# Two kernels in one program: where the load of the expert biases and the branch for crowded experts stand

## The chip, the cores and the metric

The kernel runs on one core of one Trainium2 chip. A core has a matrix engine (TensorE, PE in the profile), three elementwise engines (VectorE or DVE, ScalarE or ACT, GpSimd or POOL), a queue processor that here issues every DMA (SyncE, SP), an on-chip memory (SBUF) and accumulators (PSUM). Inputs and weights lie in HBM. The metric is the device time of one execution in microseconds (us); lower is better.

## The reference

256 tokens of width 1024 pass through two blocks in float32. The first block (four attention and convolution branches, then a gated feed-forward network) and the front of the second (pooling, differential attention, cross attention) are not touched by the change. The second block ends in a mixture of experts, and that is where the change lies:

```
logits = xt @ w_router + b_router                     # 256 tokens, 32 experts
top_val, top_idx = top_k(logits, 4); gates = softmax(top_val)
for each expert e, for the tokens xb that chose it:
    hb = clamped_swiglu(xb @ w_gu[e] + b_gu[e])       # w_gu[e]: 1024 x 2048
    yb = hb @ w_down[e] + b_down[e]                   # w_down[e]: 1024 x 1024
    y[token] += yb * gate
return rms_norm(x + y)
```

Each expert has 12 MB of weights, all 32 have 384 MB, and every one of them is read once.

## The kernel before

The work before the experts ends with the cross attention: its output product against `w_co` is added into `x_t` (the residual stream, 128 x 2 x 1024, kept on chip), the router's logits are taken, and `x_t` is added into the four PSUM accumulators `acc` (`seed`, L1337). `x_t` has no other use after that, and its space serves the experts: columns 0 to 1023 of the flat view `xa` hold an expert's gate and up values (`gs`), 1024 to 1535 its product `u_`, and the last 256 columns, `bd4`, take the down biases of all experts, which `load_b_down` brings by four small DMAs (L1422). So that load has to wait until `seed` and the scaling on POOL (L1346) have read `x_t`.

Weights come in pieces of 1 MB. A piece lies in a slot of 8 KB per partition; there are 23 slots, and the string `SLOTS` gives the order in which `slot_tile` (L1481) hands them out, round and round. An expert takes 8 pieces for gate and up (`load_gu`) and 4 for down (`load_dn`). The first two pieces of expert 0 are loaded much earlier, and 382 are left. Most slots lie on memory that the cross attention used, so the first round through the string waits for its last readers: slot h for the scores (L1225), the slots p for the splits of `w_co` (L185), d, e, i and j for the values (L1251), c for the output product (L201), b and a for the router (L1307, L1301). From the second round on a slot waits for the product that read it. The first 34 pieces are chained, each issued behind the one before (`in_turn`, L1489); the bias load is outside that chain. SP issues in order: while its first instruction waits, nothing behind it starts. Each DMA also waits until the one eight places earlier has landed.

A planner sets the order on each engine: of the instructions that it thinks ready, the one that comes first in the program goes first.

A loop runs over the experts. In the turn of expert e the gate and up product of expert e+1 is made (`front`, L1529), with the other half of the swiglu of e and the scatter of e-1 between its eight steps, and then the down product of e (L1571), which for an even e is interleaved with the gather of tokens for the next two experts. Each expert has room for 64 tokens. For experts with more there is `overflow`: a loop over all experts inside a branch, `tc.If(most > CAP)`, L1615. With these inputs no expert has more, so the loop is skipped; still each engine loads the count, branches, and on the skip path waits until its own earlier work is complete and raises its semaphores to what the other path would leave. On SP this means that all DMAs issued before have landed (eight queue semaphores). Nothing that stands behind the branch in the program is moved ahead of it, and the other way round. In the kernel before the branch stands behind all weight loads, behind the scatter of expert 29 and ahead of the swiglu of expert 30.

Of the kernel before, what the change touches and what calls it, by code (L numbers as in the profile page):

```python
# [11 lines left out]
F32 = mybir.dt.float32  # L12
# [10 lines left out]
P = 128  # L23
T = 256
D = 1024
DFF = 2816
NFC = DFF // P
NE = 32
# [15 lines left out]
def kernel(ctx: ExitStack, tc: tile.TileContext, A, out, probe=None, stop=None):  # L44
# [45 lines left out]
    def ps(name, tag="mm"):  # L90
        return pst["pool"].tile([P, 512], F32, tag=tag, name=name, bufs=pst["tags"][tag])
# [174 lines left out]
    def half(h):  # L266
        return slice(h * 512, (h + 1) * 512)
# [1047 lines left out]
    if stopped("cross"):  # L1315
# [9 lines left out]
    slots = {c: ctx.enter_context(tc.tile_pool(name=f"raw_{c}", reuse_waits="tile", bufs=1))  # L1325
             for c in sorted(set(SLOTS) - set("px"))}
# [93 lines left out]
    def load_b_down():  # L1420
        for q in range(4):
            ld(bd4[q * NE:(q + 1) * NE, :], A["b_down_2"][0, :, q * 256:(q + 1) * 256])  # L1422

    def add_b_down(odd):

        g4 = small.tile([P, 2, 4, NE], F32, tag="SG", name="g4", bufs=1)
        V.tensor_copy(g4, gate.unsqueeze(2).to_broadcast([P, 2, 4, NE]))
        gT = xa[:, 1024:1280]
        pt = ps("gT_ps", "tr")
        for b in range(2):  # L1430
            PE.transpose(pt[:, b * P:(b + 1) * P], g4[:, b].rearrange("p q e -> p (q e)"), ident)
        V.tensor_copy(gT, pt[:, :T])
        for b in range(2):
            for h in range(2):
                q = 2 * h + odd
                rows_ = slice(q * NE, (q + 1) * NE)
                PE.matmul(acc[b][h][:, odd * 256:(odd + 1) * 256], gT[rows_, b * P:(b + 1) * P], bd4[rows_, :],
                          start=False, stop=False, tile_position=(q * NE, 0))

    def one_hot(pos_cols, n, name, s_=None):  # L1440

        if s_ is None:
            s_ = small.tile([P, 2, n, 2, CAP], BF16, tag="S_", name=f"S{name}")
        io = iota_s.unsqueeze(1).unsqueeze(1).to_broadcast([P, n, 2, CAP])
        for b in range(2):
            pos = pos_cols[:, b, :].unsqueeze(2).unsqueeze(3).to_broadcast([P, n, 2, CAP])
            last["V"] = V.tensor_tensor(s_[:, b], io, pos, op=ALU.is_equal)
        return s_
# [34 lines left out]
    def slot_tile():  # L1483

        rawc[0] += 1
        pool = slots[SLOTS[slot[0] % len(SLOTS)]]
        slot[0] += 1
        return pool.tile([P, 2 * D], F32, tag="raw", name=f"raw{rawc[0]}")
# [13 lines left out]
    def dn_piece(src, k, t):  # L1502

        t = t.rearrange("p (k c) -> p k c", k=2)
        in_turn(t, src[2 * k * P:(2 * k + 2) * P, :].rearrange("(k p) c -> p k c", p=P))
        return t

    def load_gu(src, ahead=()):
        return [*ahead, *(gu_piece(src, k, slot_tile()) for k in range(len(ahead), 8))].__getitem__

    def load_dn(src, halves=False):
        w = [dn_piece(src, k, slot_tile()) for k in range(4 - halves)]
        if halves:
            t = slot_tile().rearrange("p (k c) -> p k c", k=2)
            for i in range(2):
                ld(t[:, i, :], src[(6 + i) * P:(7 + i) * P, :])
            w.append(t)
        return w.__getitem__
# [14 lines left out]
    def gu_out(pgu, name, gs=None):  # L1533
        if gs is None:
            gs = xa[:, :D]
        for n in range(2):
            S.copy(gs[:, n * 512:(n + 1) * 512], pgu[n])  # L1537
        return gs
# [36 lines left out]
    def scatter(stop=False, after=None):  # L1575

        for b in range(2):
            for y in (yh, yl):
                for h in range(2):
                    rows_ = slice(h * CAP, (h + 1) * CAP)  # L1580
                    PE.matmul(acc[b][h], sT[rows_, b * P:(b + 1) * P], y[rows_, :], start=False,  # L1581
                              stop=stop and y is yl)
            if after:
                after(b)


    GR = 2
    st = {}

    def group(g):  # L1590
        st["S", g] = one_hot(pos1[:, :, g * GR:(g + 1) * GR], GR, f"g{g}")
        st["xg"], chunk = gather(st["S", g], GR, f"g{g}")
        return chunk

    def front(e, between):
        w = load_gu(w_gu[e], () if e else gu0)
        pgu = gu_product(w, st["xg"], (e % GR) * CAP, f"e{e}", between)

        gs = slots["i"].tile([P, 2 * D], F32, tag="raw", name="gs_i")[:, :D] if e == NE - 2 else None
        return gu_out(pgu, f"e{e}", gs)  # L1600

    def slots_of(e):
        g, o = divmod(e, GR)
        st["gslot", e] = turn_slots(st["S", g][:, :, o], gate3[:, :, e, :], f"e{e}")

    chunk = group(0)
    gs = front(0, {k: [lambda k=k: chunk(k + 1)] if k else [lambda: chunk(0), lambda: chunk(1)] for k in range(7)})
    with behind({"V": last["V"]}):
        gates()
    load_b_down()  # L1610


    def overflow():
        most = nc.values_load(cnt_i[0:1, NE:NE + 1], min_val=0, max_val=T)
        with tc.If(most > CAP):  # L1615
            with tc.For_i(0, NE, 1) as e:
                ne = nc.values_load(cnt_i[0:1, bass.ds(e, 1)], min_val=0, max_val=T)
                with tc.If(ne > CAP):
                    pc = small.tile([P, 2, 1], F32, tag="pc", name="pc", bufs=1)
                    gc = small.tile([P, 2, 3], BF16, tag="gc", name="gc", bufs=1)  # L1620
                    bc = small.tile([P, 16], F32, tag="bc", name="bc", bufs=1)
                    V.tensor_copy(pc, pos1[:, :, bass.ds(e, 1)])
                    V.tensor_copy(gc, gate3[:, :, bass.ds(e, 1), :].rearrange("p b o q -> p b (o q)"))
                    V.tensor_copy(bc, bgu[:, :, bass.ds(e, 1)].rearrange("p c o -> p (c o)"))
                    wsl = [slots[c].tile([P, 2 * D], F32, tag="raw", name=f"wsl{c}") for c in "jc"]
                    oxg = work[:, :D // 2].rearrange("p (c s) -> p c s", c=8)

                    os_ = small.tile([P, 2, 1, 2, CAP], BF16, tag="S_", name="os_")

                    def piece(f, src):  # L1630
                        return lambda k: f(src, k, wsl[k % 2])

                    for blk in range(1, T // CAP):
                        V.tensor_scalar(pc, pc, float(CAP), None, op0=ALU.subtract)
                        s_ = one_hot(pc, 1, f"o{blk}", os_)
                        _, chunk = gather(s_, 1, f"o{blk}", oxg)
                        gslot = turn_slots(s_[:, :, 0], gc, f"o{blk}")
                        wg = w_gu[bass.ds(e, 1)].rearrange("o k c -> (o k) c")
                        wd = w_dn2[bass.ds(e, 1)].rearrange("o k c -> (o k) c")
                        g0 = gu_out(gu_product(piece(gu_piece, wg), oxg, 0, f"o{blk}",  # L1640
                                               {k: [lambda k=k: chunk(k)] for k in range(8)}), f"o{blk}")
                        make = swiglu(g0, bc, f"o{blk}")
                        make(0)
                        make(1)
                        dn_product(piece(dn_piece, wd), gslot, f"o{blk}")
                        scatter()

    for e in range(NE - 2):
        make = swiglu(gs, bgu[:, :, e], f"e{e}")
        make(0)  # L1650
        between = {1: [lambda: make(1)], 4: [lambda: slots_of(e)]}
        if e:
            between[3] = [lambda: scatter()]
        gs = front(e + 1, between)
        wd = load_dn(w_dn2[e])
        if e == 2:
            counts()
        chunk = group(e // GR + 1) if e % GR == 0 else None
        dn_product(wd, st["gslot", e], f"e{e}", chunk)
        if e in (2, 4):  # L1660
            add_b_down(e // 2 - 1)


    e0, e1 = NE - 2, NE - 1
    wd0, wg1, wd1 = load_dn(w_dn2[e0]), load_gu(w_gu[e1]), load_dn(w_dn2[e1], halves=True)
    scatter()
    work = slots["e"].tile([P, 2 * D], F32, tag="raw", name="work")
    gb2 = work[:, D:]
    for h in range(2):
        pt = ps(f"gb2_{h}")  # L1670
        for c in range(4):
            PE.matmul(pt[:, c * P:(c + 1) * P], vec["last"][:, 4 * h + c:4 * h + c + 1].to_broadcast([P, P]), ident,
                      start=True, stop=True)
        S.copy(gb2[:, half(h)], pt)
    overflow()
    make = swiglu(gs, bgu[:, :, e0], f"e{e0}")
    make(0)
    make(1)
    slots_of(e0)
    dn_product(wd0, st["gslot", e0], f"e{e0}")  # L1680
    pgu = gu_product(wg1, st["xg"], (e1 % GR) * CAP, f"e{e1}", {1: [scatter]})
    gs = gu_out(pgu, f"e{e1}")
# [50 lines left out]
```

## Time and profile before

| | |
|---|---|
| median of 3 runs | 1735.26 us (1732.9 to 1735.35) |
| the profiled execution | 1734.44 us |
| its span, first to last instruction | 1732.7 us |
| PE busy | 1616.9 us (93%) |
| DVE, ACT, POOL busy | 733.9, 516.5, 232.6 us |
| DMA queue of SP | 526.06 MB |
| mean granted TensorE clock | 0.990 |

A busy PE is not a PE at its peak. The chain of waits follows back from the last instruction and names at each step what released it. SPq, PEq and so on are an engine's instruction queue: semaphore, branch and DMA-issuing instructions. [...]

### The profile page before, as it was taken

Reading aid. Unit: us, or ns where it says so; the run is one execution under the profiler, and the core shown is the slowest. Engines: PE = TensorE matmul, PEld = TensorE weight load, DVE = VectorE, ACT = ScalarE, POOL = GpSimd, SP = SyncE. Lnnn points to the kernel's source line nnn. Section 1 sums busy time; section 2 is a strip of 40 time slices with the busy share of each in tenths; the row PEclk is TensorE's granted clock in tenths of the full one; section 3 lists DMA queues with packets and bytes.
Section 4 is the critical chain, followed back from the end, with each engine's and each line's share of the span. In section 5 each row is a group of like instructions: output and inputs, shape, how many; then the busy total and the mean of one; then the engine's idle time right before and its main releaser. Section 6 shows DMA issues by size and latency. Waiting matters only on the chain.

```text
span 1732.7 us, 24096 instructions
## 1 busy us (share of the span) xinstructions
PE 1616.9 (93%) x9539; PEld 974.3 (56%) x9540; DVE 733.9 (42%) x1606; ACT 516.5 (30%) x973; POOL 232.6 (13%) x332
## 2 busy tenths in 40 slices
PE   8899999999999999989999999998998988899877
PEld 8887799989999788853333333332332233233222
DVE  5867754667777775552122212221222222122122
ACT  4454554555555565531111011100100010011011
POOL 6988312200010000030000000000000000000000
PEclk9999999999999999989999999999999999999989
DMA  9851355664646545529999999999999999999994
GB/s 290 253 170 56 102 183 182 233 199 157 227 147 213 158 130 196 234 108 417 418 414 418 416 418 417 416 418 416 418 415 418 417 417 417 416 418 415 418 414 190
DMA packets 182675, 527.64 MB, mean 305 GB/s; under 512 B 13649, under 2 KB 101758, under 8 KB 149758
## 3 DMA queue, kind: packets, MB, share of 16 engines
q1 hardware_dynamic: 182558, 526.06, 79.2%
q8 instruction: 76, 1.25, 0.3%
q14 instruction: 41, 0.34, 0.1%
HBM read 524.95 MB, written 4.22 MB: 305 GB/s over the span
## 4 chain that ended last, share of the span: by engine, by line
PE 63%; DMA 26%; DVE 6%; ACT 2%; issue 2%; POOL 1%; SPq 0%; DVEq 0%; POOLq 0%; ACTq 0%
DMA raw<-in_w_gu_dram 18%; PE gue L1529 15%; DMA raw<-in_w_down_dram 8%; PE dne L1571 7%; PE dt L201 2%; PE dt L200 2%; PE dt L199 2%; PE xgg L1472 2%; PE g L193 2%; PE g L194 2%; PE g L192 2%; DVE wl L185 2%; PE acc L1581 1%; PE ffv L194 1%; PE ffv L193 1%
## 5 line engine op out<-in xcount | busy, mean ns | idle before, releaser
L1529 PE MATMUL gue<-raw,xgg 128*64 128x512 f32 x2032 | 468.9, 599 | 19.6 <-DMA raw<-in_w_gu_dram 19.6
L185 DVE TENSOR_TENSOR wl<-raw,wh 128x1024 fp32r<-128x1024 f32 (+3 forms) x218 | 273.3, 1255 | 177.5 <-ACT wh L184 177.0
L184 ACT CAST wh<-raw 128x1024 fp32r<-128x1024 f32 (+2 forms) x220 | 227.8, 1035 | 258.1 <-PE g L193 64.3
L1529 PEld LDWEIGHTS gue<-raw,xgg 128*64 128x64 f32 x2032 | 134.0, 136 | 289.4 <-issue 223.1
L1571 PE MATMUL dne<-raw,x_t 128*64 128x512 f32 x1024 | 247.3, 605 | 8.2 <-DMA raw<-in_w_down_dram 6.9
L1476 DVE TENSOR_SCALAR xgg<-xgg,v_c 128x128 f32<-128x128 f32 x120 | 42.1, 351 | 324.0 <-PE gue L1529 194.3
L1537 ACT COPY x_t<-gue 128x512 f32<-128x512 f32 x62 | 36.3, 585 | 341.4 <-PE gue L1529 341.4
L1571 PEld LDWEIGHTS dne<-raw,x_t 128*64 128x64 f32 x1024 | 64.1, 136 | 118.4 <-issue 85.7
L1697 POOL TENSOR_TENSOR ssl<-ssl,nhalf 128x1 f32<-128x1 f32 x2 | 1.1, 563 | 956.9 <-DVE ssl L1696 956.9
L1551 DVE TENSOR_TENSOR x_t<-gte,bgu 128x256 f32<-128x256 f32 x62 | 26.3, 425 | 214.6 <-ACT x_t L1537 165.0
L1472 PEld LDWEIGHTS <-xs 128*128 128x128 bf16 x768 | 46.6, 98 | 103.7 <-issue 101.6
L1472 PE MATMUL xgg<-Sg,xs 128*128 128x128 bf16 x768 | 65.3, 221 | 30.4 <-DVE xgg L1476 25.0
L209 ACT ACTIVATE yh<-dne,gslote 128x512 fp32r<-128x512 f32 x32 | 22.0, 687 | 224.7 <-PE dne L1571 224.7
L379 POOL TENSOR_TENSOR convo<-convo,prod 128x256 f32<-128x256 f32 x90 | 76.9, 854 | 7.4
L192 PE MATMUL g<-h_h,wh 128*128 128x256 f32 x256 | 73.1, 286 | 0.0
L193 PE MATMUL g<-h_l,wh 128*128 128x256 f32 x256 | 73.1, 285 | 0.0
L194 PE MATMUL g<-h_h,wl 128*128 128x256 f32 x256 | 72.9, 285 | 0.0
L1557 ACT ACTIVATE x_t<-x_t 128x256 f32<-128x256 f32 x62 | 25.8, 417 | 155.3 <-DVE x_t L1555 153.0
L378 POOL TENSOR_SCALAR prod<-hconv,v_c 128x256 f32<-128x256 f32 x90 | 66.9, 744 | 8.6
L1553 DVE TENSOR_TENSOR x_t<-gte,bgu 128x256 f32<-128x256 f32 x64 | 26.8, 419 | 79.7 <-PE dne L1571 79.7
L1545 PEld LDWEIGHTS gte<-ident,x_t 128*128 128x128 f32 x248 | 26.0, 140 | 58.3 <-issue 44.1
L194 PE MATMUL ffv<-h_h,wl 128*128 128x256 f32 x176 | 49.9, 284 | 0.2 <-DVE wl L185 0.2
(808 smaller groups left out, 3054.7 us busy)
## 6 DMA issues: line engine op xcount, KB each, us to landing
raw<-in_w_gu_dram SPq DMA_DIRECT2D x254, 1024.0 KB
raw<-in_w_down_dram SPq DMA_DIRECT2D x138, 1024.0 KB
raw<-in_w_in_dram SPq DMA_DIRECT2D x32, 1024.0 KB
raw<-in_w_up_dram SPq DMA_DIRECT2D x22, 1024.0 KB
raw<-in_w_out_dram SPq DMA_DIRECT2D x8, 1024.0 KB
raw<-in_w_ckv_dram SPq DMA_DIRECT2D x8, 1024.0 KB
raw<-in_w_in_dram SPq DMA_DIRECT2D x13, 512.0 KB
raw<-in_w_br_dram SPq DMA_DIRECT2D x12, 512.0 KB
```

The source lines that it names most:

```text
L184: S.copy(hi, src)
L185: last["lo"] = (eng or V).tensor_sub(lo, src, hi.bitcast(F32))
L192: PE.matmul(o, wh[:, k, :], ah[:, k, :], start=first and k == 0, stop=False)
L193: PE.matmul(o, wh[:, k, :], al[:, k, :], start=False, stop=False)
L194: PE.matmul(o, wl[:, k, :], ah[:, k, :], start=False, stop=last and k == nk - 1)
L378: G.tensor_scalar(prod[0][:, :T], hconv[:, c, k:k + T], w, 0.0, op0=ALU.mult, op1=ALU.add)
L379: G.tensor_add(convo[:, c, :], convo[:, c, :], prod[0][:, :T])
L1472: PE.matmul(po[:, :n * CAP], part[:, b, c * P:(c + 1) * P], s_[:, b, :, 0, :], start=i == 0, stop=i == 5)
L1476: V.tensor_scalar(xg[:, c, :], po[:, :n * CAP], vec["ffn"][:, c:c + 1], None, op0=ALU.mult)
L1529: PE.matmul(pgu[n][cg * CAP:(cg + 1) * CAP, :], xg[:, k, col:col + CAP], w[:, cg * D + n * 512:cg * D + (n + 1) * 512], start=k == 0, stop ...
L1537: S.copy(gs[:, n * 512:(n + 1) * 512], pgu[n])
L1571: PE.matmul(po[cg * CAP:(cg + 1) * CAP, :], u_[:, k // 4, k % 4, :], w[:, k % 2, cg * 512:(cg + 1) * 512], start=k == 0, stop=k == 7)
```

## The change

The down biases: `load_b_down()` stands no longer behind the first expert's gate and up product but in the turn of expert 1, behind the loads of its down weights, which is behind 32 pieces.

The branch: `overflow()` stands in the turn of expert 25 (`EOVER`), behind its down product and a scatter of its own, which is left out of the next turn. Pieces of experts 0 to 26 (gate and up) and 0 to 25 (down) are loaded ahead of the branch, the 64 others behind it. Its three tiles and the copy that keeps the gate and up values of the next expert out of its way are taken from the slots in turn instead of by name, and so is the tile for the end of the kernel.

```diff
     GR = 2
+    EOVER = NE - 7
...
-        gs = slots["i"].tile([P, 2 * D], F32, tag="raw", name="gs_i")[:, :D] if e == NE - 2 else None
-        return gu_out(pgu, f"e{e}", gs)
+        return gu_out(pgu, f"e{e}", slot_tile()[:, :D] if e == EOVER + 1 else None)
...
     with behind({"V": last["V"]}):
         gates()
-    load_b_down()
-
     def overflow():
+        wsl = [slot_tile() for _ in range(2)]
+        oxg = slot_tile()[:, :D // 2].rearrange("p (c s) -> p c s", c=8)
         most = nc.values_load(cnt_i[0:1, NE:NE + 1], min_val=0, max_val=T)
...
-                    wsl = [slots[c].tile([P, 2 * D], F32, tag="raw", name=f"wsl{c}") for c in "jc"]
-                    oxg = work[:, :D // 2].rearrange("p (c s) -> p c s", c=8)
...
-        if e:
-            between[3] = [lambda: scatter()]
+        if e and e - 1 != EOVER:
+            between[3] = [scatter]
         gs = front(e + 1, between)
         wd = load_dn(w_dn2[e])
+        if e == 1:
+            load_b_down()
...
         if e in (2, 4):
             add_b_down(e // 2 - 1)
+        if e == EOVER:
+            scatter()
+            overflow()
...
-    work = slots["e"].tile([P, 2 * D], F32, tag="raw", name="work")
+    work = slot_tile()
...
-    overflow()
     make = swiglu(gs, bgu[:, :, e0], f"e{e0}")
```

## Rows read from the trace of the kernel before

**Rows 1.** The page's 40 slices of the span: DMA busy in tenths, and GB/s.

```profile
DMA  9851355664646545529999999999999999999994
GB/s 290 253 170 56 102 183 182 233 199 157 227 147 213 158 130 196 234 108 417 418 414 418 416 418 417 416 418 416 418 415 418 417 417 417 416 418 415 418 414 190
```

**Rows 2.** Waits of SP's queue: us in total, times, longest.

```profile
SPq L1422 <- PE acc L1337: 38.9, 1, 38.9
```

**Rows 3.** Windows (us, engines, PEclk, DMA share, GB/s), 730 to 768 us.

```profile
730.00:732.00 2.00, 2.00 (x12) 1.68 (x11) 1.34 (x2) 1.41 (x3) 0.00 (x0) 1.00 0.42 176
...
734.00:764.00 30.00, 29.48 (x143) 21.08 (x142) 14.87 (x28) 12.39 (x27) 6.96 (x9) 1.00 0.00 1
764.00:768.00 4.00, 1.13 (x9) 0.77 (x9) 3.62 (x7) 1.95 (x4) 3.93 (x5) 0.75 0.09 29
```

**Rows 4.** Timeline of SP, 700 to 812 us: start us, us, what was issued.

```profile
700.11 24.85 SPq L1493 DMA_DIRECT2D raw<-in_w_gu_dram  x6
765.32 1.72 SPq L1422 DMA_DIRECT2D x_t<-in_b_down_dram  x4
767.08 2.07 SPq L1493 DMA_DIRECT2D raw<-in_w_gu_dram  x4
...
772.15 19.41 SPq L1493 DMA_DIRECT2D raw<-in_w_gu_dram  x8
```

**Rows 5.** Lines L1225, L1251, L1307: ns (min/median/max), first and last start.

```profile
L1225 PE MATMUL cs<-mk,cq__7799 x32: 378/379/483, 699.1 to 726.3; 128*128 128x256 f32 x32
...
L1251 PE MATMUL cy<-cpts,mv__3684 x32: 377/379/483, 709.0 to 740.9; 128*128 128x256 f32 x32
...
L1307 PE MATMUL lp<-ident,lsb x4: 193/276/276, 759.1 to 759.3; 128*128 128x32 f32 x4
```

**Rows 6.** Timeline of DVE and of PE, 738 to 754 us.

```profile
746.33 1.22 DVE L185 TENSOR_TENSOR wl<-raw,wh 128x1024 fp32r<-128x1024 f32 x1 [0.58 <-ACT wh L184]
...
753.60 0.39 PE L201 MATMUL dt<-wh,co_l 128*128 128x512 f32 x1
```

**Rows 7.** Chain of waits, first experts: start us, us, what.

```profile
771.52 3.61 PE gue L1529 x8
...
835.30 5.15 PE dne L1571 x24
```

**Rows 8.** Windows, the expert stage as one stretch.

```profile
767.00:1700.00 933.00, 851.91 (x4419) 301.04 (x4420) 213.38 (x601) 99.91 (x198) 3.27 (x3) 0.99 1.02 416
```

**Rows 9.** Chain of waits: down products of experts 8, 10, 24 and 28.

```profile
1033.80 1.87 PE dne L1571 x8
...
1090.03 1.87 PE dne L1571 x8
...
1511.29 1.87 PE dne L1571 x8
...
1633.07 1.87 PE dne L1571 x8
```

**Rows 10.** Line L1615, the branch: ns (min/median/max), first and last start.

```profile
L1615 SPq EVENT_SEMAPHORE  x9: 17/17/17, 1701.9 to 1711.3; - x9
...
L1615 PEldq COMPARE_BRANCH  x1: 6026/6026/6026, 1674.6 to 1674.6; - x1
...
L1615 SPq COMPARE_BRANCH  x1: 45/45/45, 1696.8 to 1696.8; - x1
```

**Rows 11.** Timeline, end of the kernel, PE.

```profile
1681.12 1.09 PE L1545 MATMUL gte<-ident,gs_i 128*128 128x128 f32 x4 [6.36 <-PEq L1615]
...
1698.14 12.24 PE L1529 MATMUL gue<-raw,xgg 128*64 128x512 f32 x56
```

**Rows 12.** Chain of waits, last down product.

```profile
1714.85 7.03 PE dne L1571 x30
```

**Rows 13.** Windows, end of the kernel.

```profile
1680.00:1690.00 10.00, 7.52 (x24) 2.92 (x26) 4.18 (x13) 1.21 (x3) 0.00 (x0) 0.62 1.01 420
1706.00:1710.00 4.00, 4.00 (x22) 1.22 (x18) 0.00 (x0) 0.43 (x1) 0.00 (x0) 1.00 0.52 204
```

## The prediction, made before the changed kernel ran

> **What bounds the kernel now.** I read the slices first. From the 18th on the DMA queue is 9 tenths busy or more and moves 413 to 418 GB/s to the end [rows 1]; as one stretch, 767 to 1700 us goes at a share of 1.02 and 416 GB/s [rows 8]. A piece of 1 MB (1.0486 million bytes) so takes 1.0486 / 0.4175 = 2.51 us, an expert's 12 pieces 30.1 us. The second view is the chain of waits. Early on PE makes its own pace: the down products of experts 8 and 10 start at 1033.80 and 1090.03, 56.2 us for a pair. Later those of 24 and 28 start at 1511.29 and 1633.07, 60.9 us for a pair, which is 24 pieces at 2.51 plus small losses [rows 9]. So PE could go 28.1 us per expert, lives on pieces loaded ahead at first, and follows the queue from about expert 12 on. What the queue loses anywhere before the last piece, or gains, reaches the end.
>
> The third view, the waits of SP, shows a large loss just ahead of this stage: the bias load stood 38.9 us for the last read of `x_t` by L1337 [rows 2]. In that time the queue moved nothing: a share of 0.42 at 730 to 732, 0.00 from 734 to 764, 0.09 up to 768 [rows 3]. SP's timeline gives the order: six pieces end at 725 (with six before them that makes 12), then the biases at 765.32, then piece 13 (slot h) at 767.08 [rows 4]. The other 11 slots of the first round stood behind the biases.
>
> **First part, the biases.** Moving them behind piece 32 lets pieces 13 to 23 go when their own slots come free. From the last readers: h at 726.7 (L1225); d, e, i and j at 741.3 (L1251); b at 759.6 (L1307) [rows 5]; the last slot p at 747.6 (L185) and c at 754.0 (L201) [rows 6]; a and the other two slots p lie between. The queue is never asked for more than it can move by then: with 2.51 us a piece and some 2.4 us from issue to first data, all 11 have landed at about 767. Piece 24 needs slot x, which is free when the first expert's first step has read it: that product starts at 771.52 and its first 8 matmul records take 3.61 us, so 775.1 [rows 7]. That start hangs on the router and the gather, not on weights, and I leave it where it is.
>
> Before, piece 13 was issued at 767.1 and everything behind it ran without a gap. After, piece 24 is issued at 775.2 and the rest follows without a gap, since PE has freed 28 slots by 835.3 [rows 7] and the queue can fill 24 of them by then. The gain is 11 pieces less the later restart: 11 x 2.51 = 27.6, less 8.1, **19.5 us**. Bounds: no gain at all if the biases keep their place in SP's order; 32 us if the queue had no gap (734 to 766), which slot x forbids. I take 19.5.
>
> The four bias loads take SP 1.72 us [rows 4] and 0.13 MB in the new place; SP is then 8 pieces ahead of the data, which hides it. The biases are first used in the turn of expert 2, ahead of which they land in any case.
>
> PE can use the gain. At expert 24 its own pace would have put the down product at 1090.03 + 7 x 56.2 = 1483.4, 27.9 us ahead of 1511.29. The queue, 19.5 us earlier, still comes last from about expert 20 on.
>
> **Second part, the branch, at its old place.** PE sat 6.03 us in the branch [rows 10] and 6.36 us went by before the next transpose at 1681.12 [rows 11]; with the stop the granted clock was 0.62 in 1680 to 1690 [rows 13]. Price of both: weights arrive until about 1710.9 (share 0.52 in 1706 to 1710 [rows 13], SP's last queue semaphores by 1711.3 [rows 10]). The last expert's four down pieces are the last 10.0 us of that, so its last gate and up piece was there at 1700.9. A step of that product takes 12.24 / 7 = 1.75 us, so it could have ended at 1702.7; it ended at 1698.14 + 12.24 = 1710.4 [rows 11]. **7.7 us** are given back if nothing else holds PE: what follows, the last swiglu, the down product that ends at 1721.9 [rows 12] and the norm, moves with it, and the last down piece is then still 3 us ahead of its use. Bounds: 0 if PE is as late by another way, 7.7 because the queue is then last.
>
> **Second part, the branch, at its new place.** On SP: the skip path waits until all DMAs issued before have landed, so the queue, 8 deep, runs dry once. SP branched at 1696.8 and raised its first semaphore at 1701.9; that is 5.1 us, most likely to fetch code, and lies under the 20 us that eight pieces in flight take. After the last landing come eight semaphores (0.35 us), one issue (0.4) and the lead from issue to data, for which the restart at 767.08 gives 1.1 us to first data and some 2.4 in all. I take **3.1 us**; bounds 1.5 (the short lead) and 8.2 (the fetch once more behind the landing).
>
> [...]
>
> On PE: scatter 25 no longer hides between steps of a product, and PE waits for its scaled result (about 1.5 us), then sits 6.4 us in the branch, then runs some 6 us at half speed (3 us lost): 11 us. Before it, expert 25's down product ends with the queue, near 1531. Pieces go on arriving meanwhile, so PE is behind the queue by 11 - 3.1 = 8 us, and each expert gives back 30.1 - 28.1 = 2.0; with the short waits that it had at expert 26 anyway, it has caught up by expert 30. I take 0 at the end, bound 4.
>
> Four slots out of 23 pass unused once (three tiles and the kept values). SP then looks 19 pieces ahead instead of 23; PE is behind by 8 us or three pieces. Nothing.
>
> **Sum.** Span 1732.7 - 19.5 - 7.7 + 3.1 = 1708.6. The execution was 1.74 us longer than its span: 1710.3. The median of the runs stood 0.82 above the profiled execution: **1711 us**.
>
> **Rivals.** (1) *SP goes on only with PE.* If a load behind the branch waits for something that PE raises on its skip path, the queue is dry from about 1529 until PE has passed at 1540, plus the restart: 13 us in place of 3.1, 1721. For it: on the skip path every engine settles its own count. Against: the slots of the first pieces behind the branch were read before it.
> (2) *The biases stay where they are.* They are outside the chain of pieces, and the planner may put them ahead of piece 13 as soon as it thinks them ready. Then only the branch counts: 1735.3 - 7.7 + 3.1 = 1731. For it: the planner put 4 of expert 1's pieces ahead of them, against the order of the text. Against: behind piece 32 all those pieces come first by right.
> (3) *Slower: the biases block SP in their new place.* `x_t` also holds the swiglu's values. If the load waits for their last use and not only for its own columns, SP stands behind piece 32 until expert 2's gate and up values are copied there, after 835 (that product ends where the next down product starts, 835.30 [rows 7]). Pieces up to 32 have landed at about 801, so the queue is dry for some 37 us: 1711 + 37 = 1748. It decides above 24 us, with a release after 822. Against: the old wait ended with L1337, though the first expert's values are written into `x_t` long after that.
> (4) *PE is last from the branch on*: a longer fetch or a longer time at half clock than 11 us; up to 1718.
>
> **Chances.** As forecast, 1704 to 1718 with (4) in it: 0.68. Rival 1: 0.13. Rival 2: 0.09. Rival 3: 0.04. The rest, mostly a better tail: 0.06. The range of 1704 to 1722 takes in rival 1 and leaves out rivals 2 and 3. No change means within 0.2%, 3.5 us, about what measurement can tell; rival 2 lies at its edge and is shared. Faster 0.90, same 0.06, slower 0.04.
>
> **What would show it.** The wait of SP at L1422 is gone or short; the share in 734 to 764 is about 0.8, with a short gap near 770; at 1500 the products stand some 19 us earlier; near 1530 there is one gap of about 3 us in the queue, PE's branch of 6 us and a stretch at the lower clock; at the end no pause ahead of expert 30, and the last gate and up product ends within 3 us of its last piece. It is wrong if the slices of the expert stage show other gaps, or if PE's steps after expert 28 no longer wait for pieces.

## The result, and the profile after

| | before | after |
|---|---|---|
| median | 1734.2 us (1732.9 to 1735.35, 4 runs) | **1710.8 us** (1708.49 to 1713.23, 4 runs) |
| profiled execution, its span | 1734.44, 1732.7 us | 1708.49, 1706.8 us |
| mean granted clock | 0.990 | 0.994 |

The ratio is 0.9865, with a 95% interval of 0.9847 to 0.9884. The forecast was 1711 us.

The page's slices, with the columns of [rows 1]. The hole that stood in the 18th slice is gone, and a dent has come in the 36th, at 364 GB/s:

```profile
DMA  9842355655554535678999999999999999999997
GB/s 283 266 161 69 106 185 185 221 189 187 189 192 165 186 122 183 259 301 348 416 417 418 415 418 416 417 417 416 418 415 419 416 417 418 416 364 417 415 415 289
```

Windows around the start of the expert stage [rows 3] (us, engines, PEclk, DMA share, GB/s). The queue now works at 0.81 where it stood still; it stops from 764 to some 773:

```profile
734.00:764.00 30.00, 27.56 (x137) 19.38 (x136) 15.95 (x31) 12.57 (x28) 9.25 (x11) 1.00 0.81 316
764.00:767.00 3.00, 0.44 (x5) 0.32 (x5) 3.00 (x5) 1.23 (x2) 3.00 (x4) 0.69 0.01 3
767.00:770.00 3.00, 1.63 (x8) 0.82 (x9) 2.86 (x9) 0.73 (x2) 0.92 (x1) 0.50 0.00 0
770.00:775.00 5.00, 5.00 (x28) 1.63 (x24) 0.57 (x3) 0.37 (x1) 0.00 (x0) 0.81 0.27 82
775.00:780.00 5.00, 5.00 (x34) 1.85 (x33) 0.00 (x0) 0.90 (x3) 0.00 (x0) 1.00 0.99 419
```

SP's timeline of that stretch [rows 4]. The group of eight that begins at 751.67 holds the wait for slot x (piece 24 goes at 772.47); the biases stand behind the down pieces of expert 1 and take 1.81 us, without a wait:

```profile
739.34 6.26 SPq L1493 DMA_DIRECT2D raw<-in_w_down_dram  x4
751.67 30.37 SPq L1493 DMA_DIRECT2D raw<-in_w_gu_dram  x8
784.01 6.85 SPq L1493 DMA_DIRECT2D raw<-in_w_down_dram  x4
790.95 1.81 SPq L1422 DMA_DIRECT2D x_t<-in_b_down_dram  x4
```

Lines of the branch [rows 10] (ns min/median/max, first and last start), now in the turn of expert 25:

```profile
L1615 SPq EVENT_SEMAPHORE  x9: 17/17/17, 1521.2 to 1532.9; - x9
...
L1615 SPq COMPARE_BRANCH  x1: 45/45/45, 1516.0 to 1516.0; - x1
...
L1615 PEldq COMPARE_BRANCH  x1: 3606/3606/3606, 1531.8 to 1531.8; - x1
```

Windows around it. From 1525 to 1535 the queue is partly dry (share 0.69, then 0.35), from 1535 to 1540 PE's granted clock is 0.51 of full speed:

```profile
1520.00:1525.00 5.00, 3.87 (x16) 0.97 (x16) 0.00 (x0) 0.16 (x1) 0.00 (x0) 1.00 1.03 415
1525.00:1530.00 5.00, 3.87 (x16) 1.06 (x16) 0.00 (x0) 0.32 (x1) 0.00 (x0) 1.00 0.69 286
1530.00:1535.00 5.00, 1.46 (x8) 0.59 (x8) 0.75 (x1) 0.36 (x1) 0.00 (x0) 0.81 0.35 90
1535.00:1540.00 5.00, 4.13 (x12) 1.49 (x12) 2.77 (x8) 0.42 (x1) 0.00 (x0) 0.51 1.02 416
1540.00:1545.00 5.00, 4.28 (x27) 1.74 (x27) 2.18 (x7) 0.79 (x2) 0.00 (x0) 1.00 1.01 424
```

PE's timeline around the branch. The first gate and up step behind it takes some 3.4 us in place of 1.94 (its first four matmul records are the last line; all eight end at 1540.3):

```profile
1527.69 1.94 PE L1571 MATMUL dne<-raw,x_t 128*64 128x512 f32 x8 [0.38 <-SPq L1615]
...
1531.20 0.73 PE L1581 MATMUL acc<-yl,sT 64*128 64x512 f32 x4
1535.87 1.08 PE L1545 MATMUL gte<-ident,raw 128*128 128x128 f32 x4 [3.94 <-PEq L1615]
1536.89 1.98 PE L1529 MATMUL gue<-raw,xgg 128*64 128x512 f32 x4
```

And at the end [rows 11]: the last step of the last gate and up product starts when its piece lands, where PE had come late to it before:

```profile
1682.52 1.94 PE L1529 MATMUL gue<-raw,xgg 128*64 128x512 f32 x8 [0.57 <-DMA raw<-in_w_gu_dram]
```

The chain of waits has the last down product at 1688.92, before at 1714.85 [rows 12]:

```profile
1688.92 7.03 PE dne L1571 x30
```

One thing has to be taken out before profiles are compared. The work ahead of the experts does not take the same time in each execution: the router's last transposes (L1307) start at 759.1 us in the profile before [rows 5] and at 756.7 in the one after, but at 759.1 again in a second profile of the changed kernel. These 2.4 us are no effect of the change. The table below therefore counts two times of each profile from that start on: when the slowest row of the last gate and up piece lands (from the trace's landing records; the queue's result), and the end of the span.

### The profile page after: what moved, and what is told of

The parts are those of the page before. It is cut to its first block, busy times and chain, and to the rows that moved or that the text cites. A ratio compares the mean times of both kernels' runs of the same rounds, so it can differ in the third digit from the quotient of the medians.

```text
span 1706.8 us, 24097 instructions
## 1 busy us (share of the span) xinstructions
PE 1604.7 (94%) x9539; PEld 972.9 (57%) x9540; DVE 734.0 (43%) x1606; ACT 516.6 (30%) x973; POOL 233.4 (14%) x332
## 5 line engine op out<-in xcount | busy, mean ns | idle before, releaser
L1529 PE MATMUL gue<-raw,xgg 128*64 128x512 f32 x2032 | 464.0, 600 | 8.7 <-DMA raw<-in_w_gu_dram 8.6
L1571 PE MATMUL dne<-raw,x_t 128*64 128x512 f32 x1024 | 243.2, 602 | 4.6 <-DMA raw<-in_w_down_dram 2.4
```

The lines of the kernel that those rows point to most:

```text
L1529: PE.matmul(pgu[n][cg * CAP:(cg + 1) * CAP, :], xg[:, k, col:col + CAP], w[:, cg * D + n * 512:cg * D + (n + 1) * 512], start=k == 0, stop ...
L1571: PE.matmul(po[cg * CAP:(cg + 1) * CAP, :], u_[:, k // 4, k % 4, :], w[:, k % 2, cg * 512:(cg + 1) * 512], start=k == 0, stop=k == 7)
```

## The experiments

| kernel | median, us | ratio to before (95%) | last gate and up piece, from L1307, us | end of span, from L1307, us |
|---|---|---|---|---|
| before | 1733.0 to 1734.2 | 1 | 941.9 | 973.6 |
| changed kernel | 1710.8 | 0.9865 (0.9847 to 0.9884) | 925.8 | 950.1 |
| the same, second time | 1709.43 | 0.9861 (0.9846 to 0.9876) | 926.5 | 950.8 |
| biases alone | 1714.25 | 0.9888 (0.9873 to 0.9903) | 923.4 | 954.9 |
| branch alone | 1728.72 | 0.9974 (0.9964 to 0.9983) | 944.6 | 968.9 |
| biases in turn 0 | 1709.16 | 0.9866 (0.9851 to 0.9881) | 925.7 | 950.1 |
| two slots less | 1727.79 | 0.9965 (0.9951 to 0.9979) | 942.2 | 968.1 |
| two slots less, first round only | 1716.6 | 0.9903 (0.9888 to 0.9918) | 931.3 | 957.3 |
| no branch | 1708.2 | 0.9849 (0.9834 to 0.9864) | 924.5 | 948.8 |
| loop's loads on POOL | 1707.8 | 0.9857 (0.9842 to 0.9872) | 923.4 | 948.1 |
| the same, branch at expert 17 | 1707.79 | 0.9857 (0.9842 to 0.9872) | 923.3 | 948.1 |
| three branches | 1720.42 | 0.9924 (0.991 to 0.9937) | 934.7 | 960.6 |
| branch at expert 29 | 1714.29 | 0.9889 (0.9874 to 0.9904) | 927.7 | 954.2 |
| the same, loads on POOL | 1717.63 | 0.9916 (0.9903 to 0.993) | 923.3 | 957.6 |

> The changed kernel as it is, as the measure for the three kernels that run beside it. Every theory: 1710.8 us within 2.

That is the second run of the changed kernel: as expected. Below, the changed kernel's 1709.4 us is this run.

### Each half of the change by itself

**Biases alone** (the kernel before, with this edit):

```diff
         gates()
-    load_b_down()
...
         wd = load_dn(w_dn2[e])
+        if e == 1:
+            load_b_down()
```

> Only the biases move; the branch stays at its old place. Theory (terms add, the queue is last): 1734.2 - 19.5 = 1714.7 us, with the branch's pause of 6 us on PE ahead of expert 30 still there and the first waits of SP as in the changed kernel. Rival A: the 2.3 us by which everything before the experts ran earlier in the changed kernel's profile belong to this part too, then 1712.4. Rival B: the old branch hides less than its price once the pieces come earlier, then below 1712 and the second part is worth nothing.

Measured 18.8 us less than the 1733.04 of the kernel before that ran beside it, 18.7 from L1307. The old branch still holds PE, by the lines of the branch:

```profile
L1614 PEldq COMPARE_BRANCH  x1: 6059/6059/6059, 1655.1 to 1655.1; - x1
```

**Branch alone** (the changed kernel, with `load_b_down()` back behind `gates()`).

> Only the branch moves, with its slots in turn; the biases are loaded at their old place, so SP stands some 39 us for the last read of x_t again. Theory: 1734.2 - 7.7 + 3.1 = 1729.6 us, one gap of about 3 us in the queue near 1550 us. Rival A: the branch costs nothing at its new place, 1726.5. Rival B: PE doesn't catch up behind the branch, 1732 to 1734.

Measured 4.3 us less than before, 4.7 from L1307; SP's wait at L1422 is 38.9 us again. 18.7 and 4.7 make 23.4, and the whole change has 23.5 and 22.8 in its two profiles: the parts add.

### Where the biases may stand

**Biases in turn 0** (`if e == 0:` in place of `if e == 1:`).

> The biases twelve pieces earlier: in the turn of expert 0, behind its down weights. They wait there for L1337 again (until some 6 us after the router's logits are turned, about 763), with the first round's last three slots behind them in SP's order. Theory (slot x decides when the stream starts for good): those three pieces go at about 765 and land by 774.5, just as piece 24 can start; the hole moves from 767 to 775 ahead to 759 to 767, and the time is that of the changed kernel, 1710.8 (0 to 1 us over it). Rival: every piece behind the waiting biases costs its 2.51 us, 1710.8 + 7.5 = 1718.

The same time as the changed kernel (1709.16 against 1709.43). SP does wait with the biases until 763.51, with three pieces of the round behind them, and the queue stands still from 758 to 764 instead of 764 to some 773. Its timeline of SP:

```profile
739.89 6.25 SPq L1493 DMA_DIRECT2D raw<-in_w_down_dram  x4
763.51 1.73 SPq L1422 DMA_DIRECT2D x_t<-in_b_down_dram  x4
765.28 17.59 SPq L1493 DMA_DIRECT2D raw<-in_w_gu_dram  x8
```

The windows (columns as above):

```profile
758.00:764.00 6.00, 4.39 (x17) 2.13 (x17) 5.55 (x16) 2.91 (x8) 5.93 (x7) 1.00 0.00 0
764.00:767.00 3.00, 0.56 (x6) 0.32 (x5) 3.00 (x4) 1.36 (x3) 3.00 (x3) 0.87 0.40 71
767.00:770.00 3.00, 1.09 (x8) 0.82 (x9) 2.93 (x8) 0.62 (x2) 1.46 (x2) 0.50 0.98 401
770.00:775.00 5.00, 5.00 (x22) 1.30 (x18) 1.04 (x5) 0.48 (x2) 0.00 (x0) 0.69 0.98 390
```

So the gain doesn't come from the wait itself, but from the pieces that are in when slot x comes free.

**Two slots less**: the round without slots b and a.

```diff
-        pool = slots[SLOTS[slot[0] % len(SLOTS)]]
+        order = SLOTS[:-2]
+        pool = slots[order[slot[0] % len(order)]]
```

> The changed kernel, but slots b and a are not used: 21 slots instead of 23 in the round. Theory (the gain of the first part is the number of pieces that land before slot x comes free): two pieces fewer are in by then, 9 instead of 11, and the end is 2 x 2.51 = 5.0 us later: 1715.8. Rival A: SP looks too few pieces ahead with 21 slots and the queue has gaps in the expert stage, 1720 and more. Rival B: these slots come free so late that the two pieces gained nothing, 1710.8.

18.4 us slower, and no test of the theory. The queue is late by the same 16 us from the first experts to the last, so it is not rival A's gaps either. SP's waits (us in total, times, longest) show one of 41.3 us ahead of the second piece of the 382, for the last read of the cross attention's values:

```profile
SPq L1494 <- PE cy L1251: 41.3, 1, 41.3
```

In the changed kernel's second profile the second to fourth of the 382 go at 688 to 690. With two slots never used, the others seem to lie elsewhere in memory, where other work has to leave first; that was not looked into.

**Two slots less in the first round only**, so that every slot stays where it is:

```diff
+        i, first = slot[0], len(SLOTS) - 2
-        pool = slots[SLOTS[slot[0] % len(SLOTS)]]
+        pool = slots[SLOTS[i if i < first else (i - first) % len(SLOTS)]]
```

> The changed kernel, slots b and a left out of the first round alone (21 slots, then all 23 in turn); all slots lie where they lay. Theory (the first part is worth 2.51 us for each piece that lands before slot x comes free): two pieces fewer, 5.0 us over the changed kernel, 1714.4. Rival A: the wait for slot x ends earlier or later with the order, so another size. Rival B: the two are worth nothing, 1709.4.

7.2 us slower than the changed kernel. Counted from L1307, its pieces land some 4.9 us later throughout the expert stage (the trace's landing records, mean of the 16 DMA rows of a piece, against the second profile of the changed kernel), and the last down product starts 4.9 us later: 2 x 2.51 = 5.0, the theory. The queue stops two pieces earlier, by the windows:

```profile
758.00:764.00 6.00, 5.29 (x26) 3.12 (x25) 4.71 (x13) 2.96 (x10) 5.30 (x6) 1.00 0.18 75
764.00:767.00 3.00, 0.78 (x9) 0.46 (x8) 2.81 (x5) 1.84 (x3) 2.94 (x3) 1.00 0.00 0
767.00:770.00 3.00, 0.00 (x0) 0.00 (x0) 3.00 (x6) 0.98 (x2) 2.59 (x3) 0.55 0.00 0
```

Of the rest 1.4 us is in the last product, whose 30 matmuls take 8.51 us in this profile instead of 7.08, at a granted clock of 0.60:

```profile
1694.00:1696.00 2.00, 1.15 (x4) 0.30 (x5) 1.94 (x7) 0.42 (x1) 0.00 (x0) 0.94 1.04 416
1696.00:1700.00 4.00, 4.00 (x16) 1.41 (x17) 0.59 (x2) 0.37 (x1) 0.00 (x0) 0.60 0.63 245
```

Why the clock fell there and not in the changed kernel, where PE's work just ahead is much the same, is open; it isn't part of the theory's 5.0.

### What the branch costs at its new place

**No branch**: `overflow()` is not called in the turn of expert 25; the loop for crowded experts is left out.

> The changed kernel without the branch: the loop for crowded experts is left out, which these inputs never enter. Theory: the branch at its new place costs the queue's gap alone, 1710.8 - 3.1 = 1707.7 us, and nothing on PE. Rival A: the mean loss over the 16 DMA rows counts, not that of the slowest, 1710.8 - 4.8 = 1706.0. Rival B: PE's pause and lower clock count too (5 us and more), 1702 to 1703. Rival C: the branch is free there, 1710.8.

**The loop's loads on POOL**: the loop, the branch and its place stay, but the weight loads inside are issued by GpSimd's queue.

```diff
+    via = [ld]
...
-            last["D"] = ld(t, src)
+            last["D"] = via[0](t, src)
...
             scatter()
+            via[0] = G.dma_start
             overflow()
+            via[0] = ld
```

> The changed kernel, but the weight loads inside the loop for crowded experts are issued by POOL and not by SP. The loop is not entered, so no load is another; but SP then has no DMA of its own inside the branch, and its skip path has no DMA to settle. Theory: the 3.1 us come from SP waiting for all landings; without that SP's 5 us at the branch lie under the eight pieces in flight, the gap in the queue goes, PE still pauses 4 to 6 us in its branch and catches up: 1707.7 us, as without a branch. Rival A: the gap comes from the branch itself (a fetch behind the landing), then 1710.8 as before. Rival B: PE's pause counts once the queue no longer stops with it: 1709 to 1711 with no gap in the queue.

Both come out at the same time, 1708.2 and 1707.8, the theory's number; beside the changed kernel's 1709.4 and 1710.8 the intervals don't part them. From L1307 the changed kernel's two profiles lie 2.0 and 2.7 us above the POOL version (1.3 and 2.0 above the one without a branch, whose queue is 1.1 later than the POOL version's from the first experts on; why is open). Lines of the POOL version's branch:

```profile
L1616 SPq COMPARE_BRANCH  x1: 50/50/50, 1516.5 to 1516.5; - x1
L1616 SPq EVENT_SEMAPHORE  x1: 17/17/17, 1517.0 to 1517.0; - x1
...
L1616 PEldq COMPARE_BRANCH  x1: 6266/6266/6266, 1532.4 to 1532.4; - x1
```

Its windows there:

```profile
1525.00:1530.00 5.00, 3.79 (x18) 1.06 (x16) 0.00 (x0) 0.00 (x0) 0.00 (x0) 1.00 1.03 425
1530.00:1535.00 5.00, 1.68 (x10) 0.60 (x8) 0.75 (x1) 0.69 (x1) 0.00 (x0) 0.82 1.02 423
1535.00:1540.00 5.00, 0.85 (x4) 0.72 (x4) 0.76 (x2) 0.00 (x0) 0.00 (x0) 0.50 1.00 410
1540.00:1545.00 5.00, 5.00 (x18) 1.53 (x18) 2.66 (x8) 0.42 (x1) 0.00 (x0) 0.65 1.00 408
```

Three things are to be seen. SP is through 0.5 us behind its branch (1516.5 to 1517.0), where it took 5.2 in the changed kernel (1516.0 to 1521.2). Those 5.2 us are no wait for a landing: the first semaphore there is that of SP's own load of the count, and pieces land at 1520.16 and 1522.60, not at 1521.2; only the second to fifth semaphore, at 1525.26 to 1532.63, come 0.02 us behind a landing each. Behind the branch the changed kernel's trace has a packet of 8 KB of instructions, from 1519.45 to 1519.77 (DMA queues, 1516.0 to 1521.3: packets, MB, share):

```profile
q14 instruction: 1, 0.01, 0.4%
```

In all twelve branches of SP with the loads on it such a packet comes, and SP goes on 1.4 us after it, 5.2 to 5.3 us behind the branch (once 3.9); with the loads on POOL it goes on after 0.2 to 0.5 us, before any such packet. By these packets it looks as if SP waits for code here, and not where its part of the loop has no loads; it wasn't tried by itself. The 5.2 us end before the landing that SP waits for next, so they cost nothing.

The queue has no gap (share 1.00 to 1.03). And PE sits 6.27 us in its branch instead of 3.61. Counted from L1307 and against the kernel without a branch, its down product starts 8.1 us late at expert 26, 3.9 at 28, 2.6 at 29, and not late at 31: some 2 us are given back per expert.

**The same at expert 17** (`EOVER = NE - 15`).

> The loop's weight loads on POOL, the branch in the turn of expert 17, where PE has fourteen experts to catch up. Theory: no drain, nothing left of PE's pause: 1707.8 us as with the branch at expert 25. Rival A: at expert 17 PE is as late as the queue and its 10 us are lost, 1715 and more. Rival B: an earlier branch is better still (under 1706).

1707.79, the theory: with fourteen experts left for PE to catch up the place costs no more than with six (the span ends 948.1 us from L1307 in both).

**Three branches**, in the turns of experts 9, 17 and 25, loads on SP:

```diff
-    EOVER = NE - 7
+    EOVER = (NE - 23, NE - 15, NE - 7)
```

with `in EOVER` for the comparisons.

> The changed kernel with the branch (and its three slots, its own scatter and the loop in it, which is not entered) three times, in the turns of experts 9, 17 and 25. Theory: each costs what the drain of the queue costs, 2.0 us (as measured against the kernel with the loop's loads on POOL) to 3.1 us (as forecast), and PE catches up behind each: 4.0 to 6.2 us over the changed kernel, 1714.8 to 1717. Rival A: the drain costs nothing where pieces lie ahead of PE (experts 9 and 17), then 1710.8. Rival B: PE's pauses and its time at the lower clock add up (10 us each), then 1725 and more.

11.0 us slower than the changed kernel. The last gate and up piece lands 8.2 us later (934.7 against 926.5; 8.9 against the first profile's 925.8), so a drain in mid-stream costs 4.1 to 4.5, more than the 2.0 to 3.1 of the theory; the last down product again takes longer, 8.41 us and not 7.08, as in the first-round kernel. It is the queue's loss: against the second profile the slowest row of a piece lands 4.2 us later behind the first drain and 8.2 behind the second. PE was 18.3 us late behind two branches, but nothing of that is left in the last products beyond the queue's 8.2; rival B is out. The window of 30 us around the first drain:

```profile
1030.00:1060.00 30.00, 28.02 (x160) 10.63 (x158) 7.64 (x22) 3.07 (x6) 0.00 (x0) 1.00 0.89 356
```

30 x (1 - 356/417) = 4.4 us lost, as a mean of the queue's 16 rows.

### The branch late

**At expert 29** (`EOVER = NE - 3`, and the scatter behind the loop over the experts falls away).

> The changed kernel with the branch four experts later, in the turn of expert 29 (behind its down product; 16 whole pieces and the last one in two halves are left). Theory (queue and PE stop together, so PE is hardly behind the queue after the drain): as the changed kernel, 1709.4 to 1712 us. Rival, the fourth of the prediction: PE's 11 us less the 3 us of the queue can't be caught up in two experts, 8 - 2 x 2.0 = 4 us, 1713.5 and more.

**The same with the loop's loads on POOL.**

> The same place (expert 29), but the loop's weight loads on POOL, so SP has nothing to settle and the queue doesn't stop. Theory: PE alone loses its 6 us in the branch and the time at the lower clock, is 8 us behind the queue and has two experts to give back 2.0 us each, so 3 to 5 us show at the end: 1711 to 1713 us, not better than with the drain. Rival: PE catches up in the waits that it would have had anyway, 1707.8.

Both are slower than their twins at expert 25, by 4.9 us (3.4 to 4.1 from L1307) and 9.8 (9.5). In the second the last gate and up piece lands at 923.3 as in its twin, so all of the 9.5 us are PE's, where 3 to 5 were expected: with only two experts left it gives none of its delay back, and its last gate and up product runs through in 12.24 us without a wait for a piece, as before the change [rows 11]:

```profile
1680.89 12.24 PE L1530 MATMUL gue<-raw,xgg 128*64 128x512 f32 x56
```

In the first the queue is 1.2 to 1.9 us later than in the changed kernel and PE the rest; the theory missed there, and its rival's 1713.5 us and more came. What the fourth rival of the prediction says is seen here, 9.5 us of PE's own; at expert 25 the delay had time to vanish (8.1 us at expert 26, none at 31). PE's branch by its line, with the queue dry in the first kernel:

```profile
L1615 PEldq COMPARE_BRANCH  x1: 3366/3366/3366, 1656.1 to 1656.1; - x1
```

and full in the second:

```profile
L1616 PEldq COMPARE_BRANCH  x1: 6086/6086/6086, 1655.4 to 1655.4; - x1
```

## Why the prediction was right

**The bound** was read rightly: where PE had experts left to catch up, what the queue lost or gained came out at the end (biases alone: 18.5 us at the last gate and up piece, 18.7 at the end).

**First part, forecast 19.5 us.** The last gate and up piece lands 18.5 us earlier with the biases alone (941.9 against 923.4), and the kernel is 18.7 to 18.8 faster. The steps are in the trace: no wait at L1422, a share of 0.81 in 734 to 764, and a hole until piece 24. That piece lands 20.4 to 20.7 us from L1307 (changed kernel, biases alone), where piece 13 landed at 13.1 before: the later restart is 7.4 to 7.6 us, forecast 8.1. Turn 0 shows that the biases' own wait doesn't count, the first round that each piece counts 2.51. The 27.6 us of the 11 pieces less that would be 20. With the biases alone the landings are 21.5 us earlier at piece 24, 18.2 at piece 36 and 18.5 at the end, so the forecast's "without a gap" was not quite so: right behind the restart the queue moves less than before (378 GB/s against 415 in 785 to 790). Rival 2, that the planner keeps the biases in front, is refuted by SP's order, rival 3 by the load at 790.95, which doesn't wait for the swiglu's values.

**The old branch, forecast 7.7 us.** In the trace of before the last gate and up piece is there at 1701.0 (forecast 1700.9); its step begins at 1698.14 + 12.24 - 1.75 = 1708.6 [rows 11], 7.6 us late. With the biases alone it is 7.2 by the same count (landing 1681.1), and the POOL version, which has no such lateness and the same queue, is 6.8 faster from L1307.

**The new place, forecast 3.1 us.** By the last piece's landing it costs 2.4 and 3.1 us (the changed kernel's two profiles against biases alone) and 2.7 (branch alone against before). The size was right, though in part by luck. The lower bound of 1.5 is a slip: its own terms, 0.35 + 0.4 + 1.1, make 1.9.

- SP's 5.1 us [rows 10], forecast as "most likely" a fetch of code and hidden under the pieces in flight, agree with that in the traces: before the change a packet of 8 KB of instructions comes from 1700.20 to 1700.51, 1.4 us ahead of the first semaphore; in the changed kernel it is 5.2 us, with the 8 KB packet in them, over before the landing that SP waits for next. The upper bound of 8.2, a second fetch behind the last landing, did not come: SP issues at 1533.02, 0.4 us behind the landing at 1532.61.
- The queue is not one server. The 16 rows of one piece landed over 7.1 us ahead of the branch and over 1.9 behind it (second profile of the changed kernel). In the drain all rows wait for the slowest: SP's issue at 1533.02 stands behind the last row's landing at 1532.61. Against the same stream without a drain (biases alone or POOL, before for branch alone) the slowest row falls 2.9 to 3.1 us back at the first piece behind it, as forecast, but 4.1 to 4.4 from the second on, about as in mid-stream. At the last gate and up piece only 2.7 to 2.9 of that are left: without a drain the rows of a piece spread further, from some 7 us at expert 25 to 8.4 to 8.7 at the end, and behind the drain they hardly do (1.7 to 2.2 at the end). So the forecast's 3.1 fits the end because two effects that it didn't have nearly cancel. The mean over the rows loses 5.3 to 5.9 (landings of the last gate and up piece), by bytes 5 x (1 - 286/417) + 5 x (1 - 90/417) = 5.5. What makes rows fall behind was not tried.

**PE behind the branch.** Forecast: 11 us late, 8 behind the queue, 2.0 given back per expert, nothing left by expert 30. The branch took 3.61 us and not 6.03; it fell into the dry queue (share 0.35 in 1530 to 1535), and so PE and queue were late together; the catching up is seen in the POOL version (some 2 us per expert). There the queue doesn't stop, so by the forecast's terms PE should be the full 11 us late; it is 8.1. The conclusion held, and the late branch shows its limit.

**Rival 1**, SP going on only with PE, is refuted: SP's first issue behind the branch is at 1533.02, PE's first matmul at 1535.87. One detail of the kernel was told wrongly ahead of the prediction: two pieces of expert 27 do go ahead of the branch on SP, between its load of the count and the branch.

**Best version.** With the loop's loads on POOL, at expert 25 or 17, the median is 1707.8 us against 1709.4 to 1710.8 for the change. The intervals overlap; that it is better rests on the profiles (2.0 to 2.7 us from L1307, and no gap in the queue).

## What to carry to other kernels

When one engine issues all loads in order, price a wait by the pieces that could have landed before the next thing that blocks anyway: 11 pieces of 2.51 us less the later hole, and nothing for the wait's own length (turn 0: the load still waits until 763.51, and the time is 1709.16 us against 1709.43). The skipped branch here made SP wait until every load before it had landed (nine semaphores, 1521.2 to 1532.9), and with the loop's loads on POOL it raised one, at 1517.0; put the loads of a rare path on a queue that the main stream doesn't use, and keep the branch so far from the end that the compute engine can give back its pause (here six experts were enough, and two were not; between them nothing was tried).

## What was not expected of the hardware

- PE's branch takes 6.02 to 6.33 us while the weight queue is full (seven branches: before, biases alone, the first two of three, and POOL at 17, 25 and 29) and 3.37 to 3.73 while it is dry (all that fell into a drain). Each of the fifteen ends 1.4 to 1.5 us after a 16 KB packet of instructions has come in; that packet starts 3.5 to 3.9 us behind the branch with the queue full and 0.9 to 1.2 with it dry. So it looks as if the branch waits for its code, and the code behind the weights; it wasn't tried by itself.
- A queue that looks saturated (416 GB/s, share 1.02) holds rows that land the same piece some 7 us apart at expert 25 and up to 8.7 at the end; stopping it there brings that to 0.6 us for the first piece behind the stop, and to 1.7 to 2.0 for the rest (the changed kernel's two profiles).
